# A squared-ReLU MLP by seven products of 2x2 blocks, its hidden activations passing through DRAM

## The chip, the cores and the metric

The kernel runs on one core of a Trainium2 chip. The metric is the device time of one execution in microseconds (us). A core has five engines that run at the same time and wait for one another by semaphores: TensorE (PE; its weight loads are shown as PEld), VectorE (DVE), ScalarE (ACT), GpSimd (POOL) and SyncE (SP, which here only issues DMAs). Each engine works through its own list of instructions in order; a DMA that stands in SP's or ACT's list waits there for its data, and what stands behind it waits too.

## What is computed

One hybrid decoder layer over 1024 tokens (SEQ) of 1024 features (D_MODEL), in float32:

```python
a = rmsnorm(h, g_mix)
conv_out, attn = ...          # gated short convolution and stick-breaking attention from a @ w_in
h = h + concat([conv_out, attn]) @ w_out
m = rmsnorm(h, g_mlp)
h = h + square(relu(m @ w_up)) @ w_down      # w_up 1024 x 4096, w_down 4096 x 1024
gate = sigmoid(rmsnorm(h, g_ple) @ w_ple_gate)
h = h + gate * (p @ w_ple_proj)
return rmsnorm(h, g_final)
```

The change concerns the fifth line, the MLP, and the two seams at which it meets its neighbours.

## The kernel before

Every float32 operand x is kept as two parts in a format that TensorE multiplies in one pass: `hi`, a rounded copy made by ACT, and `lo` = x - hi, made by DVE. `split` (L109) does both. A product is then three matmuls, hi by hi, hi by lo and lo by hi (`product_steps`, L150); each matmul is 128x128 stationary by 128x512 moving, and all terms of a sum go into one PSUM bank of 128x512. There are eight banks under four names (mm, z, tr, av; two each).

SBUF is handed out in units of 4 KB per partition from named groups, the unit that has been free longest first (`Units`, L31). A unit that is given again makes its new writer wait for its last reader.

The layer runs in this order: embedding projection, mixer norm, projections and attention (filled with work that is ready), output projection, MLP, gate. `out_second` (L825) is the second half of the output projection; for each of eight row tiles of 128 tokens it finishes the residual `h1[tt]`, which stays in SBUF until the end. Beside it `Turned` (L225) makes the MLP's input: `norm` scales a row tile on ACT and sends it to DRAM, `back` fetches it with the features spread over the partitions, `turn` finishes the transpose with four DVE transposes, and `split` multiplies by the gain and makes hi and lo. Tokens are handled in halves of 512 (h = 0 and 1): `up` for half 0 needs tiles 0 to 3 only.

The MLP goes through the 4096 hidden features in 16 groups of 256 (two blocks f of 128). `up` multiplies a group for both halves of the tokens and makes the squared ReLU as hi and lo (two ACT and two DVE instructions for each bank of 512 tokens); `down_tile` multiplies the group's 256 features by w_down for a row tile and adds the bank to `h1` with one DVE instruction. `up` of a group and `down` of the group before alternate:

```python
for g in range(2, NG):
    raw = load_up(g + 1) if g + 1 < NG else None
    wd = load_down(g)
    hid = up_units()
    for h in range(NH):
        up(hid, wu, h)
    if raw:
        wu = split_up(raw)
        down(hid_prev, wd_prev)
        hid_prev, wd_prev = hid, wd
```

The last two groups of `down` run tile by tile, with the next `Turned` (for the gate) beside them: tiles 0 to 3 are finished first, and the gate's products begin with them. The order on the engines is set by a scheduler, except on PE in the attention and on DVE in this last stretch of `down`, where it is that of the code.

## Time and profile before

| | |
|---|---|
| median of 3 runs | 1317.72 us (1317.48 to 1318.93) |
| the profiled execution: span from its first to its last instruction | 1314.3 us |
| PE busy | 1280.6 us, 97% |
| DVE, ACT, POOL busy | 827.1, 485.4, 228.9 us (63%, 37%, 17%) |
| mean granted TensorE clock | 0.998 of 2.4 GHz |

The span is what the profile of one execution shows; the runs' times hold 3.4 us more at the median (1317.72 - 1314.3). Busy PE means that matmuls are in flight: the line of a group gives their number and the mean of one from start to end, which is longer than the distance from one to the next. A wait is the idle time of an engine before an instruction and what ended it.

### The profile page before, as it was taken

The page shows a single profiled execution, that of the slowest core. Times are in us where ns is not written, and L with a number is a line of the kernel's source. Part 1 is how long each engine was busy: PE and PEld are TensorE (multiplying, and loading weights), DVE is VectorE, ACT ScalarE, POOL GpSimd, SP SyncE. Part 2 cuts the span into 40 slices and gives each one's busy share as a digit, 9 for nine tenths or more (in the row PEclk, how much of TensorE's full clock was granted, in tenths as well). Part 3 has the DMA queues.
Part 4 walks back from the last instruction along what each step waited for, and adds up shares of the span by engine and source line. Part 5 has one row for each costly group of instructions (what it writes and reads, how often), then busy time and mean ns, then how long its engine had stood idle before and what let it go on. Part 6 is the DMA issues. An engine that isn't in the chain of part 4 may idle for free.

```text
span 1314.3 us, 15437 instructions
## 1 busy us (share of the span) xinstructions
PE 1280.6 (97%) x5981; PEld 1062.9 (81%) x5981; DVE 827.1 (63%) x1248; ACT 485.4 (37%) x835; POOL 228.9 (17%) x248
## 2 busy tenths in 40 slices
PE   8999999999998999999999999999999999999997
...
GB/s 343 186 32 49 34 32 33 33 32 33 49 64 160 49 33 221 121 76 65 52 29 49 64 61 20 49 64 64 17 49 65 64 16 48 33 64 161 240 128 64
DMA packets 71377, 100.11 MB, mean 76 GB/s; under 512 B 4596, under 2 KB 52744, under 8 KB 71304
## 3 DMA queue, kind: packets, MB, share of 16 engines
...
## 4 chain that ended last, share of the span: by engine, by line
PE 71%; DVE 13%; DMA 5%; ACT 3%; issue 3%; POOL 2%; SPq 0%; ACTq 0%; POOLq 0%; DVEq 0%
PE ps_mm L155 37%; PE ps_z L155 11%; PE ps_tr L155 10%; PE ps_av L155 9%; DVE u L591 2%; PE ps_tr L605 1%; PE ps_av L635 1%; DMA u<-n_d 1%; DVE u L111 1%; DVE u L611 1%; PE ps_z L576 1%; DMA u<-in_w_ple_gate 1%; DMA n_d<-u 1%; DVE u L586 1%; DVE u L270 1%
## 5 line engine op out<-in xcount | busy, mean ns | idle before, releaser
L155 PE MATMUL ps_mm<-u,u 128*128 128x512 f32 x3000 | 716.8, 391 | 8.0 <-DVE u L218 2.6
L155 PEld LDWEIGHTS ps_mm<-u,u 128*128 128x128 f32 x3000 | 556.3, 188 | 123.8 <-DVE u L218 3.0
L110 ACT CAST u<-u 128x1024 fp32r<-128x1024 f32 x114 | 119.4, 1051 | 360.3 <-DVE u L111 279.4
L155 PE MATMUL ps_z<-u,u 128*128 128x512 f32 x792 | 198.7, 389 | 0.0
L155 PEld LDWEIGHTS ps_z<-u,u 128*128 128x128 f32 x792 | 148.6, 188 | 30.9
L857 DVE TENSOR_TENSOR u<-u 128x512 f32<-128x512 f32 x64 | 44.2, 691 | 201.3 <-ACT u L855 201.3
L155 PE MATMUL ps_tr<-u,u 128*128 128x512 f32 x660 | 164.5, 389 | 0.0
L155 PE MATMUL ps_av<-u,u 128*128 128x512 f32 (+1 forms) x660 | 161.9, 385 | 0.4 <-DVE u L139 0.4
L111 DVE TENSOR_TENSOR u<-u,u 128x1024 fp32r<-128x1024 f32 x102 | 129.7, 1273 | 38.4 <-ACT u L110 36.9
L155 PEld LDWEIGHTS ps_tr<-u,u 128*128 128x128 f32 x660 | 123.8, 188 | 25.7
L155 PEld LDWEIGHTS ps_av<-u,u 128*128 128x128 f32 x660 | 122.2, 188 | 25.6 <-DVE u L139 0.8
L120 POOL TENSOR_SCALAR me<-ms 128x1 f32<-128x1 f32 x24 | 7.5, 314 | 749.5 <-ACT u L115 749.0
L855 ACT ACTIVATE u<-ps_mm 128x512 f32<-128x512 f32 x62 | 37.0, 597 | 178.5 <-PE ps_mm L155 178.1
L593 POOL TENSOR_TENSOR u<-u,u 128x383 f32<-128x383 f32 (+5 forms) x72 | 72.9, 1015 | 108.3 <-DVE u L591 69.5
L591 DVE TENSOR_TENSOR_SCAN u<-u 128x128 f32<-128x128 f32 (+3 forms) x88 | 83.6, 950 | 2.3 <-ACT u L578 0.3
L884 DVE TENSOR_TENSOR u<-ps_z,u 128x512 f32<-128x512 f32 x88 | 60.6, 689 | 32.1 <-PE ps_z L155 31.2
L884 DVE TENSOR_TENSOR u<-ps_av,u 128x512 f32<-128x512 f32 x74 | 51.0, 689 | 37.5 <-PE ps_av L155 37.5
L884 DVE TENSOR_TENSOR u<-ps_tr,u 128x512 f32<-128x512 f32 x74 | 51.0, 689 | 35.0 <-PE ps_tr L155 34.9
L635 PEld LDWEIGHTS ps_av<-u,u 128*128 128x128 f32 x320 | 50.3, 189 | 22.4 <-DVE u L611 15.3
L635 PE MATMUL ps_av<-u,u 128*128 128x256 f32 (+1 forms) x320 | 54.6, 283 | 11.8 <-DVE u L611 11.4
L610 ACT CAST u<-ps_tr 128x512 fp32r<-128x512 f32 (+1 forms) x80 | 43.4, 543 | 58.2 <-PE ps_tr L605 57.6
L270 DVE STREAM_TRANSPOSE u<-u 128x256 f32<-128x256 f32 x80 | 46.4, 639 | 19.6 <-DMA u<-m_d 10.6
...
## 6 DMA issues: line engine op xcount, KB each, us to landing
u<-in_w_up SPq DMA_DIRECT2D x32, 512.0 KB, 3.4
u<-in_w_down SPq DMA_DIRECT2D x32, 512.0 KB, 3.5
u<-in_w_in SPq DMA_DIRECT2D x24, 512.0 KB, 4.1
u<-in_x SPq DMA_DIRECT2D x16, 512.0 KB, 8.2
pp_d<-u SPq DMA_DIRECT2D x8, 512.0 KB, 6.4
u<-in_w_out SPq DMA_DIRECT2D x8, 512.0 KB, 3.8
m_d<-u ACTq DMA_DIRECT2D x8, 512.0 KB, 2.9
u<-m_d SPq DMA_DIRECT2D x32, 128.0 KB, 3.2
```

Of the source, the lines that this page charges most:

```text
L110: nc.scalar.copy(out=hi, in_=raw)
L111: (eng or nc.vector).tensor_tensor(out=lo, in0=raw, in1=f32(hi), op=ALU.subtract)
L155: nc.tensor.matmul(ps, a, b, start=(i == 0), stop=(i == n - 1))
L270: nc.vector.transpose(self.raw[h][k][0][:, :, i * P:(i + 1) * P].rearrange("p t (b j) -> p t b j", b=4), by_tile[:, 2 * k:2 * k + 2])
L576: nc.tensor.matmul(z[:, :s1 - s0], q[:, tb * P:(tb + 1) * P], k[:, s0:s1], start=(j == 0), stop=(j == 1))
L591: nc.vector.tensor_tensor_scan(out=rev, data0=rev, data1=rev, initial=keep[:, s1:s1 + 1], op0=ALU.mult, op1=ALU.bypass)
L593: (nc.vector if s0 > 0 and pr < 3 else nc.gpsimd).tensor_tensor(out=beta[:, s0:e], in0=beta[:, s0:e], in1=keep[:, s0 + 1:e + 1], op=ALU.mult)
L610: nc.scalar.copy(out=ah[:, :w], in_=tp[:, :w])
L635: nc.tensor.matmul(av[:, t0:256], v, part[:, c0:c0 + 256 - t0], start=(j == 0 and part is ah), stop=(j == n - 1 and part is al))
L855: nc.scalar.activation(rr, ps, AF.Relu)
L857: nc.vector.tensor_tensor(out=s2, in0=rr, in1=rr, op=ALU.mult)
L884: nc.vector.tensor_tensor(out=h1[tt][0][:, ds_], in0=ps, in1=h1[tt][0][:, ds_], op=ALU.add)
```

## The change

The MLP's two products are written in the form of Strassen and Winograd: both operands are cut into 2x2 blocks, sums and differences of blocks are formed, and seven block products (P1 to P7) take the place of eight. What was one sweep over 16 groups is two:

- **up** runs through all 16 blocks n of 256 hidden features. The input m is held as seven block matrices `M` (B11, B21, B22 and the sums T1 to T4), each 4 units in hi and lo. The eighth block, B12, is needed in the sums alone. Each of the seven products of a block is a chain of 12 matmuls in a PSUM bank. P6, P7 and P4 go on adding to the bank of P1 after ACT has copied what stands in it, and P3 goes on adding to that of P5 after DVE has added it to another block. DVE and ACT then build the four blocks of the hidden activations and DVE their three sums; seven slices of 512 tokens go to DRAM (`hs_d`, 1.8 MB for each n).
- **down** runs through 32 steps (8 groups of two n by 4 token tiles `tau` of 128, each step with two row tiles, tau and tau + 4). A step loads for both n the seven slices of its 128 tokens (448 KB in pieces of 512 bytes), splits them, and does seven chains of 6 matmuls; after each, one DVE instruction adds the bank to a half of a row tile of `h1`, which was itself sent to DRAM after the output projection and fetched again.
- the weights are prepared block by block (`prep_up`, `prep_down`): four block sums on POOL, then four splits on ACT and DVE (one of 512, three of 1024 elements).
- PE's order from the output projection to the last chain is that of the code. The row tiles are finished in the order 0, 4, 1, 5, 2, 6, 3, 7 in the last four steps, and the gate takes them in that order.

```diff
+    def prep_up(r):
+        a11, a21 = r[0][0][:, :, 0:P], r[0][0][:, :, P:256]
+        a12, a22 = r[1][0][:, :, 0:P], r[1][0][:, :, P:256]
+        one = W(F32R, (P, 2, 4, P))
+        split(a11, one[0][:, 0], one[0][:, 1])
+        hi, lo = W(F32R, (P, 4, 256)), W(F32R, (P, 4, 256))
+        split(r[1][0], hi[0], lo[0])
...
+        s, q = W(F32, (P, 2, 4, P)), W(F32, (P, 2, 4, P))
+        add(s[0][:, 0], a21, a22, nc.gpsimd)
+        sub(s[0][:, 1], s[0][:, 0], a11, nc.gpsimd)
+        sub(q[0][:, 0], a11, a21, nc.gpsimd)
+        sub(q[0][:, 1], a12, s[0][:, 1], nc.gpsimd)
+        free(*r)
+        for u, names in ((s, ("P5", "P6")), (q, ("P7", "P3"))):
+            hi_, lo_ = W(F32R, (P, 2, 4, P)), W(F32R, (P, 2, 4, P))
+            split(u[0], hi_[0], lo_[0])
...
+    def up(n, name):
...
+        chain(ps, [(lh(t), ll(t), rh(t), rl(t)) for t in range(4)], name in FRESH)
+        held.used()
+        if name == "P1":
+            s["A"] = W(F32, (P, 2, HB))
+            nc.scalar.copy(out=s["A"][0][:, 0], in_=ps)
+        elif name == "P2":
+            a11 = s["A"][0][:, 0]
+            add(a11, ps, a11)
+            relu2(a11)
+        elif name == "P6":
+            nc.scalar.copy(out=s["A"][0][:, 1], in_=ps)
+        elif name == "P7":
+            s["B"] = W(F32, (P, 2, HB))
+            a22 = s["B"][0][:, 0]
+            nc.scalar.copy(out=a22, in_=ps)
+            add(a22, s["V"], a22)
+            relu2(a22)
+        elif name == "P3":
...
+            add(a21, ps, a21)
+            relu2(a21)
+            s["C"], s["D"] = W(F32, (P, 2, HB)), W(F32, (P, 2, HB))
+            c, d = s["C"][0], s["D"][0]
+            add(c[:, 0], a21, a22)
+            sub(c[:, 1], c[:, 0], a11)
+            sub(d[:, 0], a11, a21)
+            for src, i, w in ((a11, 0, HB), (c.rearrange("p a b -> p (a b)"), 1, S)):
+                nc.sync.dma_start(out=hs_d[n * P:(n + 1) * P, i * HB:i * HB + w], in_=src)
+        elif name == "P4":
+            a12, c, d = s["B"][0][:, 1], s["C"][0], s["D"][0]
+            nc.scalar.activation(a12, ps, AF.Relu)
+            nc.vector.tensor_tensor(out=a12, in0=a12, in1=a12, op=ALU.mult)
+            sub(d[:, 1], a12, c[:, 1])
+            for src, i in ((d, 3), (s["B"][0], 5)):
+                nc.sync.dma_start(out=hs_d[n * P:(n + 1) * P, i * HB:(i + 2) * HB],
+                                  in_=src.rearrange("p a b -> p (a b)"))
...
+        gained(1)
+        (b11, b21), (b12, b22) = [(mT.raw[h][0:2], mT.raw[h][2:4]) for h in range(2)]
...
+        t1 = combine(sub, b12, b11)
+        free(*b11)
+        m_block("T1", t1)
+        up(2, "P1")
+        up(2, "P2")
+        t2 = combine(sub, b22, t1)
...
+        for n in range(3):
+            up(n, "P5")
...
+        for n in range(3, NP_):
+            m = n + 1
+            more = m < NP_
+            up(n, "P6")
+            if more:
+                up(m, "P1")
+                up(m, "P2")
+            up(n, "P7")
+            if m + 1 < NP_:
+                ups[m + 1] = prep_up(raws.pop(m + 1))
+                if m + 2 < NP_:
+                    raws[m + 2] = load_up(m + 2)
+            if more:
+                up(m, "P5")
+            up(n, "P3")
+            up(n, "P4")
...
+    def load_hidden(n, tau):
+        r = W(F32, (P, 7, P))
+        nc.sync.dma_start(out=r[0], in_=hs_d[n * P:(n + 1) * P].rearrange("f (i t) -> f i t", i=7)
+                          [:, :, tau * P:(tau + 1) * P])
+        hi, lo = W(F32R, (P, 7, P)), W(F32R, (P, 7, P))
+        split(r[0], hi[0], lo[0])
...
+    def down(k, name):
...
+        chain(ps, ops, name in FRESH)
...
+        top, low = h1[tau][0], h1[tau + 4][0]
+        out_ = {"P1": top[:, 0:HB], "P2": top[:, 0:HB], "P6": top[:, HB:S], "P3": top[:, HB:S],
+                "P4": low[:, 0:HB], "P5": low[:, HB:S], "P7": low[:, HB:S]}[name]
+        add(out_, ps, out_)
...
+    nT = Turned(h1, G_PLE, n_d, "W", "W", ORDER, "W")
...
+        for k in range(last + 1):
+            ahead(k)
+            down(k, "P6")
+            if k < last:
+                down(k + 1, "P1")
+                down(k + 1, "P2")
+            down(k, "P7")
+            if k < last:
+                down(k + 1, "P5")
+            down(k, "P3")
+            down(k, "P4")
+            g, tau = steps_[k]
+            if g == NP_ // GP - 1:
...
+                if tau:
+                    nT.turn(tau - 1)
+                    nT.turn(tau + 3)
+                nT.norm(tau)
+                nT.norm(tau + 4)
+    for k_ in range(4):
+        nT.split(0, k_)
```

`prep_down` has the form of `prep_up`; `relu2` is one DVE instruction, max(x, 0) times x. In the rows that follow a name's second number counts buffers and has no meaning of its own. L111 is the subtraction in `split`, L817 and L820 are `add` and `sub` of the changed kernel (L817 with a `ps_` operand takes a PSUM bank out), L900 is `relu2`.

**Where the output projection meets up, DVE.** Before, the last `turn` (tile 7, L270) is followed by the splits of half 1 (L279), between squared-ReLU work of the first groups (L857, L858):

```order
L270 STREAM_TRANSPOSE u450_4923<-u461_4998 128x2x128
L270 STREAM_TRANSPOSE u451_4924<-u461_4998 128x2x128
L270 STREAM_TRANSPOSE u452_4925<-u461_4998 128x2x128
L270 STREAM_TRANSPOSE u453_4926<-u461_4998 128x2x128
L279 SCALAR_TENSOR_TENSOR u474_5110<-u450_4923,gp_91,u473_5109 128x512 x2
L279 SCALAR_TENSOR_TENSOR u476_5116<-u451_4924,gp_91,u475_5115 128x512 x2
L279 SCALAR_TENSOR_TENSOR u478_5122<-u452_4925,gp_91,u477_5121 128x512 x2
L857 TENSOR_TENSOR u472_5100<-u472_5100 128x512
L279 SCALAR_TENSOR_TENSOR u480_5128<-u453_4926,gp_91,u479_5127 128x512 x2
```

In the changed kernel the last transpose of tile 7 (L272) is followed by the lo part of a weight block, P2 of block 2, and the sums T1, T2 and T3 (L820); the two rows with which this piece ends are the lo parts of T1:

```order
L272 STREAM_TRANSPOSE u454_4946<-u462_5015 128x2x128
L111 TENSOR_TENSOR u484_5131<-u480_5121,u483_5130 128x1024
L817 TENSOR_TENSOR u493_5171<-ps_av_5173,u493_5171 128x512
L820 TENSOR_TENSOR u487_5146<-u451_4943,u426_4714 128x1024
L820 TENSOR_TENSOR u488_5147<-u452_4944,u427_4715 128x1024
L900 SCALAR_TENSOR_TENSOR u493_5171<-u493_5171 128x512
L820 TENSOR_TENSOR u494_5188<-u453_4945,u487_5146 128x1024
L820 TENSOR_TENSOR u451_4943<-u453_4945,u451_4943 128x1024
L820 TENSOR_TENSOR u495_5189<-u454_4946,u488_5147 128x1024
L820 TENSOR_TENSOR u452_4944<-u454_4946,u452_4944 128x1024
L111 TENSOR_TENSOR u491_5152<-u487_5146,u489_5150 128x1024
L111 TENSOR_TENSOR u492_5153<-u488_5147,u490_5151 128x1024
```

Work that took no part in the seam before (four block sums) now stands between the last transpose and T1, which the first P5 multiplies.

**In the steady part of up, DVE.** Before, one stretch of a group reads so (L884 is the bank of `down`, L111 a weight's lo part):

```order
L884 TENSOR_TENSOR u415_4552<-ps_av_7087,u415_4552 128x512
L111 TENSOR_TENSOR u631_7116<-u629_7113,u630_7115 128x1024
L884 TENSOR_TENSOR u415_4552<-ps_z_7095,u415_4552 128x512
L857 TENSOR_TENSOR u636_7148<-u636_7148 128x512
L858 TENSOR_TENSOR u633_7120<-u636_7148,u632_7119 128x512
L111 TENSOR_TENSOR u641_7244<-u624_7103,u640_7243 128x1024
```

In the changed kernel P2 of one block is taken out, squared, two lo parts of weights follow, and then the bank of P5 is added at P7 (the fifth row), which P3 waits for on PE; the last row is P3's own bank:

```order
L817 TENSOR_TENSOR u574_5857<-ps_av_5859,u574_5857 128x512
L900 SCALAR_TENSOR_TENSOR u574_5857<-u574_5857 128x512
L111 TENSOR_TENSOR u582_5904<-u579_5897,u581_5903 128x1024
L111 TENSOR_TENSOR u584_5908<-u580_5898,u583_5907 128x1024
L817 TENSOR_TENSOR u575_5886<-ps_tr_5780,u575_5886 128x512
L900 SCALAR_TENSOR_TENSOR u575_5886<-u575_5886 128x512
L817 TENSOR_TENSOR u559_5722<-ps_tr_5780,u559_5722 128x512
```

The two rows of weights have moved in front of an addition for which PE waits; before, nothing on PE waited for `lo` rows of a weight until a group later.

**Where up meets down, DVE.** Before, `down`'s first banks are taken out between rows of `up` (L884 in the third row):

```order
L111 TENSOR_TENSOR u503_5316<-u489_5176,u502_5315 128x1024
L857 TENSOR_TENSOR u499_5306<-u499_5306 128x512
L884 TENSOR_TENSOR u368_4026<-ps_z_5319,u368_4026 128x512
L858 TENSOR_TENSOR u469_5010<-u499_5306,u468_5009 128x512
L111 TENSOR_TENSOR u508_5454<-u506_5451,u507_5453 128x1024
```

In the changed kernel this is the end of a piece of 30 rows between the last row of block 14 and the first bank of `down` (the last row here); lo parts of weights (1024) and of the hidden slices (896) for the first four steps make up most of it:

```order
L820 TENSOR_TENSOR u713_7196<-u711_7177,u712_7195 128x512
L111 TENSOR_TENSOR u786_7554<-u784_7551,u785_7553 128x896
L111 TENSOR_TENSOR u749_7297<-u745_7287,u748_7296 128x1024
L111 TENSOR_TENSOR u737_7270<-u735_7267,u736_7269 128x896
L111 TENSOR_TENSOR u778_7486<-u776_7483,u777_7485 128x896
L111 TENSOR_TENSOR u772_7422<-u768_7412,u771_7421 128x1024
L111 TENSOR_TENSOR u740_7276<-u738_7273,u739_7275 128x896
L817 TENSOR_TENSOR u714_7220<-ps_z_7300,u714_7220 128x512
```

The bank of P1 of the first step is taken out behind all of them, and P6, which adds to the same bank, stands behind that on PE.

## Rows read from the trace of the kernel before

**Rows 1.** The page's first part: busy us, share, count of each engine.

```profile
PE 1280.6 (97%) x5981; PEld 1062.9 (81%) x5981; DVE 827.1 (63%) x1248; ACT 485.4 (37%) x835; POOL 228.9 (17%) x248
```

**Rows 2.** Chain that ended last, a step in the MLP: start, us, engine, bank.

```profile
587.61 21.76 PE ps_mm L155 x96
```

**Rows 3.** Windows: busy us of each engine, clock, DMA share, GB/s.

```profile
core 0: us, PE busy (x) PEld busy (x) DVE busy (x) ACT busy (x) POOL busy (x), PEclk, DMA share, GB/s
500.00:550.00 50.00, 49.48 (x218) 40.46 (x217) 39.81 (x65) 29.18 (x42) 3.93 (x11) 1.00 0.62 189
1000.00:1050.00 50.00, 50.00 (x222) 41.42 (x221) 25.45 (x34) 11.54 (x16) 0.00 (x0) 1.00 0.20 69
1200.00:1250.00 50.00, 49.77 (x219) 40.55 (x217) 39.74 (x62) 28.30 (x43) 4.72 (x12) 1.00 0.70 211
150.00:200.00 50.00, 47.92 (x260) 40.48 (x259) 45.64 (x81) 29.19 (x58) 20.45 (x19) 1.00 0.11 32
```

**Rows 4.** Groups by form, 600 to 1150: busy us, mean ns of one.

```profile
L111 DVE TENSOR_TENSOR u<-u,u 128x1024 fp32r<-128x1024 f32 x51 | 62.4, 1224 | 7.4 <-ACT u L110 6.5
L110 ACT CAST u<-u 128x1024 fp32r<-128x1024 f32 x51 | 53.6, 1051 | 280.6 <-DVE u L111 256.4 <-DMA u<-in_w_down 12.6 <-DVE u L858 11.6
L884 DVE TENSOR_TENSOR u<-ps_z,u 128x512 f32<-128x512 f32 x77 | 53.1, 690 | 27.0 <-PE ps_z L155 26.1
```

**Rows 5.** Timeline of PE, 454 to 465, rows of the output projection among attention's.

```profile
454.76 0.62 PE L155 MATMUL ps_z<-u,u 128*128 128x512 f32 x2
...
464.58 0.39 PE L155 MATMUL ps_z<-u,u 128*128 128x512 f32 x1
```

**Rows 6.** Groups by form, 488 to 552, where the MLP's input is made.

```profile
L270 DVE STREAM_TRANSPOSE u<-u 128x256 f32<-128x256 f32 x32 | 18.7, 643 | 10.7 <-DMA u<-m_d 10.6
...
L278 ACT ACTIVATE u<-u,gp 128x512 fp32r<-128x512 f32 x16 | 10.2, 711 | 6.5 <-DVE u L270 6.1 <-ACT u L240 0.4
L240 ACT ACTIVATE u<-u,rs 128x1024 f32<-128x1024 f32 x8 | 9.1, 1149 | 4.9 <-POOL rs L123 4.9
L115 ACT ACTIVATE u<-u 128x1024 f32<-128x1024 f32 x8 | 8.5, 1057 | 14.7 <-DVE u L715 9.0 <-DMA m_d<-u 5.2 <-DVE u L270 0.5
```

**Rows 7.** DMA issues: count, KB each, median us from issue to landing.

```profile
u<-in_w_up SPq DMA_DIRECT2D x32, 512.0 KB, 3.4
...
m_d<-u ACTq DMA_DIRECT2D x8, 512.0 KB, 2.9
u<-m_d SPq DMA_DIRECT2D x32, 128.0 KB, 3.2
n_d<-u ACTq DMA_DIRECT2D x8, 512.0 KB, 3.9
u<-n_d SPq DMA_DIRECT2D x32, 128.0 KB, 3.4
```

**Rows 8.** Windows around an idle stretch of PE, columns as in rows 3.

```profile
400.00:404.00 4.00, 1.73 (x11) 1.22 (x9) 3.98 (x6) 0.63 (x3) 2.84 (x4) 1.00 0.45 131
404.00:406.00 2.00, 2.00 (x9) 1.71 (x7) 1.99 (x1) 2.00 (x5) 2.00 (x1) 0.60 0.03 8
406.00:408.00 2.00, 2.00 (x8) 1.60 (x8) 1.93 (x4) 1.17 (x2) 2.00 (x2) 0.55 0.36 106
```

**Rows 9.** Timeline, 565 to 567: a chain of six and its bank's addition.

```profile
565.69 1.52 PE L155 MATMUL ps_z<-u,u 128*128 128x512 f32 x6
567.48 0.68 DVE L884 TENSOR_TENSOR u<-ps_z,u 128x512 f32<-128x512 f32 x1
```

**Rows 10.** Timeline of POOL and DVE, 391 to 401.

```profile
391.00 1.09 POOL L593 TENSOR_TENSOR u<-u,u 128x511 f32<-128x511 f32 x1
393.75 6.36 POOL L111 TENSOR_TENSOR u<-u,u 128x1024 fp32r<-128x1024 f32 x2 [0.55 <-ACT u L110]
...
394.56 3.31 DVE L524 SCALAR_TENSOR_TENSOR u<-u,gc,u 128x1022 f32<-128x1022 f32 x1
397.79 0.55 DVE L611 TENSOR_TENSOR u<-ps_tr,u 128x384 fp32r<-128x384 f32 x1
398.26 2.94 DVE L111 TENSOR_TENSOR u<-u,u 128x1024 fp32r<-128x1024 f32 x1
```

More of the change, by code (lines that the diff above doesn't have):

```diff
@@ L225, in hybrid_layer_kernel, with __init__ @@
     class Turned:
-        def __init__(self, src, gcol, hn_d, raw="A", row="R"):
+        def __init__(self, src, gcol, hn_d, raw="A", row="R", order=range(8), out="A"):
+            self.order, self.out_group = list(order), out
             self.src, self.gcol, self.hn_d, self.raw_group, self.row_group = src, gcol, hn_d, raw, row
@@ L263, in turn @@
         def turn(self, tt):
-            h, i = tt // 4, tt % 4
+            at = self.order.index(tt)
+            h, i = at // 4, at % 4
             if i == 0:
@@ L794, in split_half, with W @@
         return a, b
-    G = 2
-    NG = 32 // G
-    def load_up(g):
-        r = [U.get("W", F32, (P, 4, 256)) for _ in range(2)]
+    for f in SECOND[len(y2):]:
+        y2.append(split_unit(Y[f], "VY"))
+    for g in list(U.free_q):
+        if g != "W":
+            U.move(g, "W", len(U.free_q[g]))
+    NP_ = 16
+    h_d = dpool.tile([S, D], F32, name="h_d")
+    hs_d = dpool.tile([NP_ * P, 7 * HB], F32, name="hs_d")
+    mm_steps = product
+    def W(dtype, shape=(P, S)):
+        return U.get("W", dtype, shape)
@@ new lines, in free, with add, sub, __init__ @@
+    def free(*us):
+        for u in us:
+            U.put(u, "W")
+    def add(out, a, b, eng=None):
+        (eng or nc.vector).tensor_tensor(out=out, in0=a, in1=b, op=ALU.add)
+    def sub(out, a, b, eng=None):
+        (eng or nc.vector).tensor_tensor(out=out, in0=a, in1=b, op=ALU.subtract)
+    class Held:
+        def __init__(self, units, uses):
+            self.units, self.left = units, uses
+        def used(self):
+            self.left -= 1
+            if not self.left:
+                free(*self.units)
@@ new lines, in hybrid_layer_kernel, with new_bank, chain @@
+    RIGHT = {"P1": "B11", "P2": "B21", "P5": "T1", "P6": "T2", "P7": "T3", "P3": "B22", "P4": "T4"}
+    FRESH = ("P1", "P2", "P5")
+    BANKS = {"X": ("mm", "z"), "V": ("tr", "av")}
+    turns = {"X": 0, "V": 0}
+    def new_bank(kind):
+        turns[kind] += 1
+        return bank(BANKS[kind][turns[kind] % 2])
+    def chain(ps, ops, fresh):
+        n = 3 * len(ops)
+        i = 0
+        for lh, ll, rh, rl in ops:
+            for a, b in ((lh, rh), (lh, rl), (ll, rh)):
+                nc.tensor.matmul(ps, a, b, start=(fresh and i == 0), stop=(i == n - 1),
+                                 skip_group_check=not fresh)
+                i += 1
@@ L825, in out_second @@
+    mT = Turned(h1, G_MLP, m_d, raw="W", row="W")
+    raws = {n: load_up(n) for n in range(2)}
     def out_second(tt):
@@ new lines, in hybrid_layer_kernel, with ahead @@
+    ORDER = (0, 4, 1, 5, 2, 6, 3, 7)
+    nT = Turned(h1, G_PLE, n_d, "W", "W", ORDER, "W")
+    wg = []
+    def ahead(k):
+        if k + 1 < len(steps_):
+            g, tau = steps_[k + 1]
+            hidden[k + 1] = [load_hidden(g * GP + p_, tau) for p_ in range(GP)]
+        g, tau = steps_[k]
+        if (g + 1) * GP < NP_:
+            if tau in (0, 2):
+                dr.append(load_down((g + 1) * GP + tau // 2))
+            else:
+                n = (g + 1) * GP + tau // 2
+                downs[n] = prep_down(dr.pop(0))
```

301 lines of the change are left out of this document (169 added, 132 removed).

## The prediction

> **What bounds the kernel now.** The first view is the page's table of busy time [rows 1]: PE is busy for 97% of the span, DVE for 63%, ACT 37%, POOL 17%. The chain that ended last tells why: through the MLP it is matmuls alone, 96 of them in 21.76 us [rows 2], so one matmul costs 21.76 / 96 = 0.2267 us. The windows say where the other engines have room [rows 3]: in the middle of the MLP (1000 to 1050) PE is busy for all 50 us, DVE for 25.45, ACT for 11.54, POOL for none. At both of the MLP's ends PE is nearly full as well, 49.48 of 50 us where the MLP's input is made and 49.77 where the gate begins: seams that cost nothing. So time is saved here only by fewer matmuls, and lost only where PE is made to wait.
>
> **The change part by part.** Times are of the profiled execution, 1314.3 us; the runs' median is 3.4 us above it, which is added at the end.
>
> *Fewer matmuls.* Before, up and down have 16 x 96 = 1536 matmuls each. After, up has 16 x 7 x 12 = 1344 and down 32 x 7 x 6 = 1344. 384 fewer by 0.2267 us [rows 2] is **-87.0**. The rest of the sum is what PE waits for.
>
> *Attention's tail.* Before, the output projection's second half already fills holes of the attention: 16 matmuls between 454.76 and 464.58 [rows 5], 3.6 us. In code order they come afterwards. Bounds 0 and 3.6, and the holes are partly others' anyway: **+2**.
>
> *Front seam.* I follow PE's new row order from the first matmul of `out_second` (time 0). PE has eight tiles of 24 matmuls (43.5 us) and six chains of 12 (P1 and P2 of three blocks, 16.3): 59.8. P1(0) waits for B11's lo parts, which queue on DVE among transposes and evictions (2.3 by the row order), and P1(2) for a weight's lo part (3.1): the cover ends at 65.2. P5(0) needs T1, and T1 needs tile 7. Its residual is there at 44.2; on ACT some 10 us of casts and gains (1.05 and 0.71 each [rows 4, 6]) stand ahead of its norm; norm, scaling and pass through DRAM take 1.06 + 0.5 + 1.15 [rows 6] + 2.9 + 3.2 [rows 7] = 8.8; two lo parts ahead 2.4 and four transposes by 0.643 [rows 6] 2.6: 68.0. Then 1.4 of gain, and on DVE six sums, a relu2 and two lo parts, 6 x 1.224 + 0.69 + 2 x 1.224 [rows 4] = 10.5: 79.9, 14.7 after the cover ends. Before, half 0 alone was enough to begin; T1 is a difference of both halves. After idle PE runs slow for a while: after the gap at 400 to 404 the granted clock was 0.60 and 0.55 for the next 4 us [rows 8], at those shares 1.7 us lost, called 2. With 1.4 less for gaps that were there before: 2.3 + 3.1 + 14.7 + 2 - 1.4 = **+21** (16 to 26, by the queue's length on ACT).
>
> *Steady up.* A block takes PE 84 x 0.2267 = 19.04 us. DVE, ACT and POOL need 12.3, 6.2 and 4.4 of these, by the durations of [rows 4] and POOL's 1.09 for a sum of 512 [rows 10]. PE has one tight spot: P3 adds to the bank of P5 and must wait until DVE has added that bank to another block. In DVE's order this addition stands behind the eviction and squaring of P2 and two lo parts of weights. P2's matmuls are through at 8.16 us of the cycle (three chains of 2.72); with 0.43 us of latency [rows 9], then 0.69 + 0.69 + 1.22 + 1.22 + 0.69, it ends at 13.1, and P3 is due after five chains, at 13.6: some 0.4 us of slack. What takes it is POOL. When POOL and DVE both work on SBUF they don't overlap freely: two POOL subtractions of 1024 took 6.36 us while a DVE instruction took 3.31, and a DVE lo part beside the second took 2.94 where 1.224 is usual; a DVE copy out of PSUM between them kept its 0.55 [rows 4, 10]. In up, POOL's four sums for the block after the next start when the second raw weight tile lands. Its load (3.4 us [rows 7]) stands on SP behind the writes of the hidden blocks and lands 9 to 11 us into the cycle, right where those lo parts run. A stall is between 0 and 2.7 us per block; each of up to three SBUF instructions of DVE can be held by up to 1.09, half of it on average, less the slack: about 1.0, in some 12 blocks, **+12** (0 to 30).
>
> The Trainium skill, SBUF — State Buffer, section Who interferes with whom, says that GpSimd and DVE share a port pair under an exclusive lock, that a DVE instruction with two SBUF inputs contends with a GpSimd instruction that reads SBUF, and one with at most one SBUF input doesn't. The trace agrees: 2.94 against 1.224 us, and 0.55 unchanged [rows 10]. It speaks against this change, whose sums on POOL all read SBUF; by it the sum stays where it is, without it POOL's part of the terms would be 0 and the sum that of the first rival.
>
> *Mid seam.* 30 rows stand on DVE between the last row of block 14 and the first bank of down, most of them lo parts of 1024 (1.224) and of 896 (1.09, interpolated between 0.69 and 1.224 [rows 4]): 28.8 us. P6 of step 0 adds to the bank of P1 and waits for them: it starts 34.8 us after P4(14), where PE has 15 us of chains: 19.8. Twelve POOL sums run beside these rows (+4), the clock falls once (+2 [rows 8]), and block 15's share of up's stalls is counted here (-2): **+24** (17 to 32).
>
> *Down.* Four steps take PE 28 x 6 x 0.2267 = 38.1 us. DVE has in them 28 evictions by 0.69 [rows 4], eight lo parts of hidden slices by 1.09, and two weight blocks by 0.69 + 3 x 1.224: 19.3 + 8.7 + 8.7 = 36.7, 96% of PE's time and in fixed order. P7 and P4 wait for the eviction three chains earlier, P6 for one six earlier, P3 for one eight earlier. Walking the 28 chains with these waits and 0.43 us of latency [rows 9] gives 40.5 us per group. POOL's eight sums hold DVE by some 0.4 each after what is hidden: about 43. Some six of the eight groups are full (the first has its blocks ready, the last prepares none): 6 x 2.4 = 15 without POOL's part, 6 x 4.7 = **+28** with it. Bounds: 6 (DVE's rests hidden, one stall per group) to 60 (every sum holds DVE for its whole 1.09).
> The loads are no limit: a step reads 896 KB in 9.5 us, 95 GB/s, with the weights 150; pieces of 512 bytes moved 32 GB/s at a share of 0.11 in the last row of [rows 3], about 290 at a full share.
>
> *Tail.* The gate's first half needs tiles 0, 4, 1, 5; from the last addition to tile 5 PE has two steps of cover, 19 us. Behind it come two norms (1.06 + 1.15 each with POOL's power between), out and back (3.9 + 3.4 [rows 7]), eight transposes (5.1), eight splits, and turns stand ahead of evictions on DVE, which holds PE earlier. The walk has the first gate product at 46.5 where 30.6 would be without waits; with the clock **+17** (10 to 22).
>
> Sum: 1314.3 - 87.0 + 2 + 21 + 12 + 24 + 28 + 17 = 1331.3; with 3.4, **1335 us**. The saving goes into three seams (62) and into DVE's fixed order (40).
>
> **Rivals.**
> *POOL's sums cost nothing:* they fall beside evictions, which POOL doesn't disturb [rows 10], or into DVE's rests. Then up 0, mid 20, down 15: -87 + 2 + 21 + 0 + 20 + 15 + 17 = -12, **1306 us, faster**. This is the one that ends on the other side. Its place is P3's wait in up and P7's and P4's in down; it decides when all stalls by POOL come to less than about 13 us, 0.3 us per block in up and 1 per group in down. For it: DVE is 65% busy in up. Against: in down 96%.
> *The seams are half hidden and down keeps PE's pace:* half of 62, nothing else beyond 5: -87 + 31 + 5 = -51, **1267 us**. For it: before, the seams cost almost nothing [rows 3]. Against: T1 and the 30 rows can't be earlier in DVE's order.
> *POOL and DVE run strictly one after the other:* up's stall 2.7 by 15, down 60: -87 + 2 + 24 + 40 + 28 + 60 + 19 = +86 less 18 where POOL waits behind DVE instead, **1386 us**.
>
> **How the numbers follow.** The forecast has a chance of 0.55 (its own range 1320 to 1352), the free POOL 0.29 (1295 to 1318), half-hidden seams 0.07, the serial case 0.09. A measurement here tells about 0.2%, 2.6 us, from no change. Faster: 0.07 + 0.26 of the second case (its upper edge reaches no change): 0.33. Same: 0.03 of that case and 0.05 of the forecast's lower edge, 0.08. Slower: 0.50 + 0.09 = 0.59. The range, 1280 to 1372, leaves out most of the two extreme cases (0.16 together) and a little of the forecast's upper tail.
>
> **What the profile after would show.** PE idle of 15 to 20 us before P5(0), released by DVE's lo part of T1; of some 20 us before P6 of step 0, released by the first L817 of down; of 10 us or more before the gate. In up a cycle of 20 us, not 19.04, with idle before P3 released by the L817 of P7's addition; L111 on DVE well above 1.224 us there. In down a group of four steps of 43 us, PE waiting for L817. Granted clock below 1 after each long gap. POOL's sums above 1.09. Wrong would be: L111 at 1.22 and POOL at 1.09 beside each other (then 1306), seams below 8 us each, or SP's queue, not DVE, as what ended PE's waits.

## Result and the profile after

The changed kernel takes 1362.72 us (median of 4 runs, 1359.1 to 1366.45) against 1318.33 for the kernel before: ratio 1.0335 (95% interval 1.0311 to 1.036), slower by 44.4 us where 17 were forecast. The sign was right and the size was not. Its profiled execution spans 1363.0 us, 48.7 more than the one before.

The page's first part, of after, answers to [rows 1]:

```profile
PE 1229.8 (90%) x5597; PEld 1004.3 (74%) x5597; DVE 1035.4 (76%) x1414; ACT 565.7 (42%) x913; POOL 439.7 (32%) x376
```

PE does 384 matmuls less and is busy for 51 us less, yet the span has grown. So the time is in waits of PE, and in slower matmuls behind some of them. Its list of waits, of after (what waited, for which engine and line, us in all, times, the longest):

```profile
PE ps_z L895 <- ACT u L110: 32.3, 4, 19.5
PE ps_tr L895 <- DVE u L817: 23.3, 13, 5.1
...
PE ps_z L895 <- DVE u L817: 8.4, 6, 1.9
PE ps_tr L895 <- ACT u L110: 7.0, 1, 7.0
PE ps_z L895 <- DVE u L111: 6.4, 2, 4.4
```

L895 is the matmul of `chain`. Thirteen waits for L817 are P3's, one in nearly every block; the long ones for L110 (a split's cast) are the seams. A number in brackets behind a product is its block: P5(0) is P5 of block 0. To see what each stage lost I take the time between two matmuls and subtract 0.2267 us for each matmul between them. The landmarks are rows of PE's timeline of after:

```profile
522.23 2.88 PE L155 MATMUL ps_av<-u,u 128*128 128x512 f32 x12
531.24 0.79 PE L895 MATMUL ps_z<-u,u 128*128 128x512 f32 x1 [6.13 <-ACT u L110]
...
571.68 5.06 PE L895 MATMUL ps_tr<-u,u 128*128 128x512 f32 x11 [4.10 <-DVE u L111]
...
892.57 2.88 PE L895 MATMUL ps_mm<-u,u 128*128 128x512 f32 x12
914.96 1.22 PE L895 MATMUL ps_z<-u,u 128*128 128x512 f32 x2 [19.50 <-ACT u L110]
920.60 0.79 PE L895 MATMUL ps_z<-u,u 128*128 128x512 f32 x1 [4.42 <-DVE u L111]
925.16 1.92 PE L895 MATMUL ps_z<-u,u 128*128 128x512 f32 x3 [3.77 <-ACT u L110]
926.88 2.66 PE L895 MATMUL ps_av<-u,u 128*128 128x512 f32 x6
...
1265.94 0.73 PE L155 MATMUL ps_mm<-u,u 128*128 128x512 f32 x2 [3.83 <-ACT u L280]
```

The first is the end of the output projection (525.0); 571.45 is where P5(0)'s first matmul would begin if it stood right ahead of the other eleven; 895.3 is the end of up, 926.88 the second chain of down, 1265.94 the gate. For the front seam that is 571.45 - 524.95 - 6 x 2.72 = 30.2. In the same way, for after and for the runs that are told below (us that PE lost; "down" ends 16 chains before the gate):

| run | front | up | mid | down | tail |
|---|---|---|---|---|---|
| forecast | 21 | 12 | 24 | 28 | 17 |
| after | 30.2 | 35.5 | 30.2 | 17.2 | 18.5 |
| no sums | 23.9 | 5.7 | 16.5 | 8.4 | 19.8 |
| sums on POOL, unused | 26.6 | 37.0 | 28.9 | 36.3 | 19.3 |
| sums on DVE | 22.9 | 9.9 | 24.4 | 13.8 | 19.8 |
| P4 first | 29.5 | 7.2 | 29.3 | 15.4 | 18.5 |
| w_up loads on ACT | 28.5 | 50.7 | 30.4 | 13.6 | 18.5 |
| sums on DVE, P4 first | 23.6 | 5.4 | 28.9 | 15.6 | 18.9 |

One block of up shows the mechanism. First DVE's timeline, of after, then POOL's and one row of ACT's, in the same stretch:

```profile
759.12 0.69 DVE L820 TENSOR_TENSOR u<-u 128x512 f32<-128x512 f32 x1
759.72 2.31 DVE L111 TENSOR_TENSOR u<-u,u 128x1024 fp32r<-128x1024 f32 x1
761.96 1.77 DVE L820 TENSOR_TENSOR u<-u,u 128x512 f32<-128x512 f32 x1
763.65 0.68 DVE L944 TENSOR_TENSOR u<-u 128x512 f32<-128x512 f32 x1
764.37 1.67 DVE L820 TENSOR_TENSOR u<-u,u 128x512 f32<-128x512 f32 x1
767.53 0.69 DVE L817 TENSOR_TENSOR u<-ps_av,u 128x512 f32<-128x512 f32 x1 [1.50 <-PE ps_av L895]
...
771.25 2.42 DVE L111 TENSOR_TENSOR u<-u,u 128x1024 fp32r<-128x1024 f32 x2 [2.30 <-ACT u L110]
773.58 0.68 DVE L817 TENSOR_TENSOR u<-ps_tr,u 128x512 f32<-128x512 f32 x1
```

```profile
759.34 1.60 POOL L817 TENSOR_TENSOR u<-u,u 128x512 f32<-128x512 f32 x1 [12.97 <-PE ps_z L895]
761.02 2.16 POOL L820 TENSOR_TENSOR u<-u,u 128x512 f32<-128x512 f32 x1
763.86 1.62 POOL L820 TENSOR_TENSOR u<-u 128x512 f32<-128x512 f32 x1 [0.68 <-issue]
765.44 1.74 POOL L820 TENSOR_TENSOR u<-u,u 128x512 f32<-128x512 f32 x1
```

```profile
770.16 2.24 ACT L110 CAST u<-u 128x1024 fp32r<-128x1024 f32 x2 [4.83 <-DMA hs_d<-u]
```

POOL's four sums begin as soon as P4 of the block is through (a unit comes free then), not when a weight tile lands. Beside them a lo part takes 2.31 us instead of 1.22 and two subtractions 1.77 and 1.67 instead of 0.69: each loses about what a sum of POOL takes alone, 1.09 [rows 10], 3.15 us per block. The rows that I had expected to be held (771.25) run at their usual 1.21 each, but late: they waited 2.30 us for ACT's cast, and the cast 4.83 us for a write of hidden activations to DRAM (`hs_d`). The chain that ended last, of after, from the block before, shows how the loss gets there (start, us, what):

```profile
739.00 2.23 DVE u L111
741.22 1.71 DVE u L820
742.95 0.32 SPq L940
...
743.38 0.38 SPq L836
...
743.85 5.47 DMA hs_d<-u
...
749.42 1.06 ACT u L110
...
750.51 2.36 DVE u L111 x2
752.87 0.61 DVE u L817
...
753.53 3.03 PE ps_tr L895 x12
```

A held lo part and a held subtraction make the hidden block late, and with it its writes: L940, and L947, which stands behind L940 and a load of w_up (L836) in SP's list. L947's write lands 5.47 us after its issue, and only then the cast begins; it makes a part of the weights in a unit that the hidden block has held until then. Two lo parts, the addition of P7, and only then P3. The casts do not wait for the load of w_up. ACT's waits of after, from 600 to 850:

```profile
ACT u L110 <- DMA hs_d<-u: 51.2, 15, 5.2
...
ACT u L110 <- DMA u<-in_w_up: 4.2, 2, 2.7
```

The load counts in another way, beside the write. One block later than the last load of w_up, rows of DVE are held for as long as in the block above (2.31, 1.78 and 1.67 us), but the cast begins 3.5 us after L947's issue (848.31), and P3 waits for 0.32 us and not for 1.5:

```profile
851.82 2.21 ACT L110 CAST u<-u 128x1024 fp32r<-128x1024 f32 x2 [2.54 <-DMA hs_d<-u]
...
857.13 3.01 PE L895 MATMUL ps_tr<-u,u 128*128 128x512 f32 x12 [0.32 <-DVE u L817]
```

A block takes 20.8 to 22.4 us instead of 19.04, this last one aside.

### The profile page after: what moved, and what is told of

It reads as the page before. It is cut to its first block, busy times and chain, and to the rows that moved or that the text cites. A ratio compares the mean times of both kernels' runs of the same rounds, so it can differ in the third digit from the quotient of the medians.

```text
span 1363.0 us, 15562 instructions
## 1 busy us (share of the span) xinstructions
PE 1229.8 (90%) x5597; PEld 1004.3 (74%) x5597; DVE 1035.4 (76%) x1414; ACT 565.7 (42%) x913; POOL 439.7 (32%) x376
## 4 chain that ended last, share of the span: by engine, by line
PE 39%; DVE 20%; issue 16%; DMA 10%; POOL 8%; ACT 4%; SPq 1%; POOLq 0%; ACTq 0%; DVEq 0%
PE ps_mm L155 16%; DVE u L111 7%; POOL u L820 6%; PE ps_tr L895 5%; DMA hs_d<-u 5%; DVE u L820 3%; PE ps_tr L155 3%; PE ps_z L155 3%; PE ps_av L155 3%; PE ps_mm L895 2%; DVE u L817 2%; PE ps_z L895 2%; DVE u L593 2%; PE ps_av L637 2%; ACT u L110 2%
## 5 line engine op out<-in xcount | busy, mean ns | idle before, releaser
L110 ACT CAST u<-u 128x1024 fp32r<-128x1024 f32 (+2 forms) x256 | 242.2, 970 | 405.8 <-POOL u L820 103.6
L155 PE MATMUL ps_mm<-u,u 128*128 128x512 f32 (+1 forms) x1464 | 365.1, 395 | 10.2 <-ACT u L280 3.8
L111 DVE TENSOR_TENSOR u<-u,u 128x1024 fp32r<-128x1024 f32 (+2 forms) x244 | 305.7, 1268 | 72.5 <-ACT u L110 70.0
L155 PEld LDWEIGHTS ps_mm<-u,u 128*128 128x128 f32 x1464 | 269.4, 190 | 65.5 <-ACT u L280 4.2
L895 PE MATMUL ps_z<-u,u 128*128 128x512 f32 x768 | 200.7, 404 | 47.5 <-ACT u L110 32.3
L895 PE MATMUL ps_tr<-u,u 128*128 128x512 f32 x756 | 190.6, 402 | 34.4 <-DVE u L817 23.3
L895 PEld LDWEIGHTS ps_z<-u,u 128*128 128x128 f32 x768 | 147.7, 194 | 86.7 <-ACT u L110 34.1
L895 PE MATMUL ps_mm<-u,u 128*128 128x512 f32 x768 | 192.9, 393 | 13.0 <-ACT u L110 5.7
L895 PEld LDWEIGHTS ps_tr<-u,u 128*128 128x128 f32 x756 | 145.2, 194 | 71.3 <-DVE u L817 28.8
L895 PEld LDWEIGHTS ps_mm<-u,u 128*128 128x128 f32 x768 | 144.5, 189 | 47.4 <-DVE u L817 6.5
L820 POOL TENSOR_TENSOR u<-u,u 128x512 f32<-128x512 f32 x80 | 137.8, 1732 | 38.3 <-DMA hs_d<-u 35.6
L820 POOL TENSOR_TENSOR u<-u 128x512 f32<-128x512 f32 x32 | 47.3, 1480 | 236.3 <-PE ps_mm L895 137.5
L895 PE MATMUL ps_av<-u,u 128*128 128x512 f32 x396 | 101.7, 401 | 0.0
L817 DVE TENSOR_TENSOR u<-ps_tr,u 128x512 f32<-128x512 f32 x95 | 63.6, 684 | 45.9 <-PE ps_tr L895 41.1
L895 PEld LDWEIGHTS ps_av<-u,u 128*128 128x128 f32 x396 | 77.7, 196 | 16.8
L817 POOL TENSOR_TENSOR u<-u,u 128x512 f32<-128x512 f32 x16 | 25.2, 1573 | 200.4 <-PE ps_z L895 79.3
L637 PEld LDWEIGHTS ps_av<-u,u 128*128 128x128 f32 x320 | 50.1, 189 | 24.9 <-DVE u L613 18.1
L637 PE MATMUL ps_av<-u,u 128*128 128x256 f32 (+1 forms) x320 | 54.8, 284 | 13.7 <-DVE u L613 13.2
L272 DVE STREAM_TRANSPOSE u<-u 128x256 f32<-128x256 f32 x80 | 46.1, 635 | 26.1 <-DMA u<-m_d 19.8
```

The source lines that it names most:

```text
L110: nc.scalar.copy(out=hi, in_=raw)
L111: (eng or nc.vector).tensor_tensor(out=lo, in0=raw, in1=f32(hi), op=ALU.subtract)
L155: nc.tensor.matmul(ps, a, b, start=(i == 0), stop=(i == n - 1))
L272: nc.vector.transpose(self.raw[h][k][0][:, :, i * P:(i + 1) * P].rearrange("p t (b j) -> p t b j", b=4), by_tile[:, 2 * k:2 * k + 2])
L637: nc.tensor.matmul(av[:, t0:256], v, part[:, c0:c0 + 256 - t0], start=(j == 0 and part is ah), stop=(j == n - 1 and part is al))
L817: (eng or nc.vector).tensor_tensor(out=out, in0=a, in1=b, op=ALU.add)
```

## Experiments

**No sums on POOL.** In `prep_up` and `prep_down` the four sums go, and the raw tiles are split in their place (the result is then not the layer's); `prep_up` is shown:

```diff
-        add(s[0][:, 0], a21, a22, nc.gpsimd)
-        sub(s[0][:, 1], s[0][:, 0], a11, nc.gpsimd)
-        sub(q[0][:, 0], a11, a21, nc.gpsimd)
-        sub(q[0][:, 1], a12, s[0][:, 1], nc.gpsimd)
-        free(*r)
-        for u, names in ((s, ("P5", "P6")), (q, ("P7", "P3"))):
+        for u, names in ((r[0], ("P5", "P6")), (r[1], ("P7", "P3"))):
...
```

> The 128 block sums on POOL are left out (up and down); the two raw tiles of a block are split in their place, so the weights of P3, P5, P6, P7 (in down P4 to P7) are not the right ones, with the same casts, lo parts and matmuls. Theory lock: DVE's SBUF instructions beside POOL cost 1.05 to 1.1 us more each, 3.1 us per block in up, 8 us in the mid seam; without them up has a cycle of 19.3 us instead of 20.9, the mid seam shrinks from 30 to about 20, a group of down from 40.1 to 39: about 1325 us, L111 at 1.22 and L820 at 0.69 all through. Theory queue: P3 waits because the weight tile is loaded behind the hidden blocks' writes; the order on SP stays, so the cycle stays above 20.3 and the time above 1345. Theory fixed order (DVE's list, not POOL): above 1350.

Measured: 1304.1 us, 0.9893 (0.9879 to 0.9908): 58.6 us less than the changed kernel, more than theory lock had, and theory queue is out: SP's order did change, but one load of w_up goes out as P6's copy begins (729.18 and 729.38) and the other only 7.7 us after it (737.07), where it was 4.5 in the block above, and still P3 waits no more between 600 and 845 us. The windows from 600 to 850, of this run and then of after, have PE busy for 247.88 and 228.41 of 250 us:

```profile
600.00:850.00 250.00, 247.88 (x1087) 204.66 (x1085) 144.91 (x194) 74.66 (x102) 0.00 (x0) 0.99 0.49 175
```

```profile
600.00:850.00 250.00, 228.41 (x975) 185.00 (x974) 176.16 (x180) 70.63 (x95) 85.49 (x50) 0.98 0.40 141
```

The 128 sums on POOL cost, by stage, 6.3 us in the front seam, 29.8 in up, 13.7 in the mid seam and 8.8 in down (the table's second row less the third), and nothing in the tail. But the run differs in three more things: casts need no sums, a block holds two units less, and the scheduler has ordered DVE anew. One lo part, and not two, stands ahead of P7's addition (the second row):

```profile
736.99 1.23 DVE L111 TENSOR_TENSOR u<-u,u 128x1024 fp32r<-128x1024 f32 x1 [0.68 <-ACT u L110]
738.22 0.69 DVE L817 TENSOR_TENSOR u<-ps_tr,u 128x512 f32<-128x512 f32 x1
```

The next run tells the first apart, and the run with the sums on DVE, which has all the units in use and is nearly as fast in up, speaks against the second. The order was not varied by itself: it has one lo part ahead of that addition in the three runs in which up is short (no sums, sums on DVE, P4 first), and two in the changed kernel and in the next run.

**The same sums on POOL, used by nobody.** As above, with the four POOL instructions put back (the diff is against the run above); weights are still split from the raw tiles, so no instruction waits for a sum's value, though a unit still comes free only when POOL has read it.

```diff
+        s, q = W(F32, (P, 2, 4, P)), W(F32, (P, 2, 4, P))
+        add(s[0][:, 0], a21, a22, nc.gpsimd)
...
+        free(s, q)
         for u, names in ((r[0], ("P5", "P6")), (r[1], ("P7", "P3"))):
```

> POOL makes all its block sums as in the changed kernel, but nobody uses them: the weights are split from the raw tiles, as in the run without sums (1304.1 us), so nothing waits for a result of POOL and its adds stand in nobody's way but the port's. Theory lock: DVE is held as before, and most of the 58.6 us between the two runs come back: above 1340 us, L820 and L111 on DVE at 1.5 us or more in up. Rival, the wait for POOL's results (its sums are late, so casts and lo parts are): the time stays below 1312.

Measured: 1380.41 us, 1.0471 (1.0451 to 1.049). All of it came back, and 18 us more, mostly in down. Theory lock holds: nobody need wait for a sum's value for POOL's work to cost this. DVE's groups by form, from 620 to 860, of this run:

```profile
L111 DVE TENSOR_TENSOR u<-u,u 128x1024 fp32r<-128x1024 f32 x33 | 51.9, 1588 | 28.5 <-ACT u L110 28.5
L820 DVE TENSOR_TENSOR u<-u,u 128x512 f32<-128x512 f32 x22 | 37.8, 1720 | 0.4
...
L817 DVE TENSOR_TENSOR u<-ps_tr,u 128x512 f32<-128x512 f32 x24 | 16.5, 688 | 32.8 <-PE ps_tr L896 32.8
```

and of the run without sums, where the same rows read

```profile
L111 DVE TENSOR_TENSOR u<-u,u 128x1024 fp32r<-128x1024 f32 x34 | 41.5, 1221 | 10.7 <-ACT u L110 10.7
...
L820 DVE TENSOR_TENSOR u<-u,u 128x512 f32<-128x512 f32 x24 | 16.4, 685 | 0.1
```

L820 between two SBUF operands takes 1720 ns against 685; L817 out of PSUM takes 688 here and 692 there. That POOL stretches these rows is so shown; that the stretch reaches P3 is shown by the chain above. How up's 29.8 us divide between the stretch and the second lo part in front of the addition is not: by the rows of the block above (an estimate) the two held rows are 2.2 us longer (2.31 and 1.77 against 1.22 and 0.69), more than P3's usual wait of 1.5 us, and a lo part is 1.22, somewhat less than it. Why this run is slower than the changed kernel itself was not followed.

**The sums on DVE.** `nc.gpsimd` is left out of the eight calls, so that DVE makes the sums.

```diff
-        add(s[0][:, 0], a21, a22, nc.gpsimd)
+        add(s[0][:, 0], a21, a22)
...
```

> All block sums of the weights run on DVE instead of POOL, four of 0.69 us for each block. Theory lock: POOL's sum stops DVE for about 1.08 us, more than the 0.69 that DVE needs itself, so up and the mid seam get no worse and rather better: 1340 to 1360 us. Rival, DVE as the bound: 2.76 us more on DVE per block in up and per block in down (two per group: 36.7 + 5.5 = 42.2 us of DVE against 38.1 of PE), so a group of down goes to 43 or more and the time to 1370 to 1385.

Measured: 1320.79 us, 1.0021 (1.0011 to 1.0031): 41.9 us faster than the changed kernel, better than theory lock had. To do the work itself takes DVE 0.68 us for a sum; to have POOL do it beside it cost up to 1.09. A group of down goes at 39.8 us (977.42 to 1017.24 between the same waits), not 43: the rival, DVE as the bound, is out, although DVE works 5.5 us more.

**P4 ahead of P3 in up.** P4's part takes ReLU and square only, the sums and writes follow P3; shown is the loop, the first three blocks change likewise:

```diff
-            up(n, "P3")
             up(n, "P4")
+            up(n, "P3")
```

> In up P4 runs ahead of P3, so that the addition of P5's bank at P7, for which P3 waits, has one chain (2.72 us) more. Theory: up's 1.85 us per block are P3's wait alone, for whatever reason that addition is late; they go, some 12 blocks, and the clock's dips in up with them: a cycle of 19.1 to 19.4 us, 1335 to 1342 us. Rival: the wait only moves (to P6 or P1 of the next block, whose banks DVE or ACT then frees later, or to the last block's hidden slices, which are written 2.7 us later, at the mid seam): above 1352.

Measured: 1331.63 us, 1.0099 (1.0084 to 1.0114), 31.1 us faster than the changed kernel. Up falls from 35.5 to 7.2 us while POOL still works 80.57 us beside it: POOL still stretches rows of DVE (L817 with both operands in SBUF takes 1442 ns on average from 620 to 860, and 692 without sums), and one chain of slack keeps it from PE. The window from 600 to 850, of this run:

```profile
600.00:850.00 250.00, 249.31 (x1100) 206.12 (x1099) 169.47 (x198) 72.72 (x102) 80.57 (x49) 1.00 0.47 169
```

**Loads of w_up issued by ACT.**

```diff
-            nc.sync.dma_start(out=r[k][0], in_=w_up[:, n * 256:(n + 1) * 256]
+            nc.scalar.dma_start(out=r[k][0], in_=w_up[:, n * 256:(n + 1) * 256]
```

> The loads of w_up are issued by ACT instead of SP, so that they no longer stand behind the writes of the hidden blocks, which wait for DVE. Theory queue: the second raw tile lands 3 to 5 us earlier, its lo parts no longer stand late in front of the addition at P7, P3's wait of 1.5 us goes: about 1340 us with POOL's sums as they are. Theory lock alone: POOL's sums still stretch DVE, and the time stays above 1355.

Measured: 1372.46 us, 1.0412 (1.0396 to 1.0427), slower by 9.7. In ACT's list the two loads stand behind two copies out of PSUM: in the block whose P6 ends at 766.8 they go out at 766.84 and 769.56, 0.0 and 2.7 us after the start of P6's copy. In the block of the changed kernel shown above it is 2.2 and 4.5 us (764.18 and 766.48, the copy at 762.02). So the loads are some 2 us earlier in the block, and yet up lost 50.7 us instead of 35.5: an earlier load does not shorten P3's wait, and theory queue fails here too. The casts ahead of P3 wait for the writes of the hidden block again:

```profile
774.02 1.05 ACT L110 CAST u<-u 128x1024 fp32r<-128x1024 f32 x1 [3.88 <-DMA hs_d<-u]
776.95 1.05 ACT L110 CAST u<-u 128x1024 fp32r<-128x1024 f32 x1 [1.88 <-DMA hs_d<-u]
```

The second ends 11.2 us after P6's copy begins, where it was 10.4 (770.16 and 2.24, less 762.02), and P3's wait grows from 1.46 to 2.24 us. The load now runs beside the second write; that it makes this write late fits the block without a load, but was not tried by itself.

**Sums on DVE and P4 first together.**

> Sums on DVE and P4 ahead of P3 together. Alone they gave 41.9 and 31.1 us. In up both remove the same waits of P3 (35.5 us of waits in the changed kernel, 9.9 and 7.2 with one of the two): theory, they overlap, up comes to about 5 us, the seams and down stay as with the sums on DVE: 1312 to 1318 us. Rival: two separate losses, which add up: 1290 to 1297.

Measured: 1322.23 us, 1.0031 (1.0019 to 1.0043), no better than the sums on DVE alone, and above the range of the theory. The two remedies take away the same loss, in up (9.9, 7.2 and 5.4 us); against the sums on DVE alone the mid seam is 4.5 us longer and down 1.8.

**Hidden slices ahead of h1.** On top of the last one, `hidden[0]` gets its units first and the loads of the eight row tiles of h1 come last before the first chain:

```diff
-    del h1[:]
-    for tt in range(8):
-        h1.append(W(F32))
-        nc.sync.dma_start(out=h1[tt][0], in_=h_d[tt * P:(tt + 1) * P])
...
+        hidden[0] = [load_hidden(p_, 0) for p_ in range(GP)]
         dr = [load_down(0)]
```

> As the one before, and where down begins the hidden slices and weights of the first step take the units that are free first, ahead of the eight row tiles of h1 (which are needed only when the first bank is taken out). Theory: the mid seam is long because the first hidden slices wait for units that block 15 still holds, so that their loads stand behind its writes on SP; the seam shrinks by 8 to 15 us. Rival: the 30 rows on DVE ahead of the first bank set it; then less than 3 us.

Measured: 1312.82 us, 0.9956 (0.9939 to 0.9974): 9.4 us less than the run before it, and the first version with all its sums that is faster than the kernel before. The first chain of down no longer waits; PE's waits move to the next two, for casts and lo parts of weights and then (879.16) for casts of hidden slices:

```profile
865.09 0.80 PE L895 MATMUL ps_av<-u,u 128*128 128x512 f32 x1 [6.87 <-ACT u L110]
870.50 1.22 PE L895 MATMUL ps_av<-u,u 128*128 128x512 f32 x2 [4.61 <-DVE u L111]
879.16 0.79 PE L895 MATMUL ps_tr<-u,u 128*128 128x512 f32 x1 [6.16 <-ACT u L110]
```

So units and SP's order had a part, some 9 us. The three waits that are left, 17.6 us, are for ACT's casts and DVE's lo parts; how much of them DVE's 30 rows set was not tried.

**Another order of the last eight steps.** On top of sums on DVE and P4 first; the loads of the last weights, the turns and the gate's weights are moved to fit, the last to the end of step 29, behind the gate's first splits:

```diff
-    steps_ = [(g, tau) for g in range(NP_ // GP) for tau in range(4)]
+    steps_ = [(g, tau) for g in range(6) for tau in range(4)]
+    steps_ += [(g, tau) for half in ((0, 1), (2, 3)) for g in (6, 7) for tau in half]
```

> Sums on DVE, P4 first, and the last eight steps of down in another order: token tiles 0 and 1 of both last groups first, so that row tiles 0, 4, 1, 5 are finished four steps (38 us) before the gate instead of two. Theory: the tail's 18.5 us are the way of tile 5 through norm, DRAM, turn and split, for which two steps are too short; with four they fall to 3 or less, while the last group's weights are prepared within two steps and cost some 4 us: 10 to 15 us faster than the run with sums on DVE and P4 first. Rival: DVE's list, with turns and splits in front of evictions, sets the tail whatever the cover: less than 4 us.

Measured: 1337.81 us, 1.0149 (1.0127 to 1.0171), 15.6 us slower than the version that it was made from. PE waits for casts of the gate's weights, which come late,

```profile
PE ps_mm L155 <- ACT u L110: 11.6, 2, 7.6
```

and from the gate's first matmul to the end it takes 121.7 us instead of 96.8; 13 of the difference are 58 matmuls of down that now run behind that first matmul. Whether units run short, with two groups' weights held at once, or the gate's weights are late by their new place alone was not followed, and whether more cover alone would help is left open.

**The gate's weights one step later.** Sums on DVE, P3 ahead of P4, hidden slices ahead of h1, and:

```diff
-                if tau == 1:
+                if tau == 2:
                     U.free_q["G"] = deque()
```

> Sums on DVE, P3 ahead of P4 as in the changed kernel, hidden slices ahead of h1 at the start of down, and the gate's weights take their units one step later, behind the hidden slices of the last step. Theory: in the tail PE waits twice (5.3 and 3.2 us) for the last step's hidden slices, whose units stand in line behind the gate's weights; these waits go and the tail falls from 19.8 to 10 to 13; with 9 us of the mid seam, from the 1320.8 us of the run with sums on DVE: 1302 to 1308. Rival: the gate's own weights are then late, and the tail only changes its name: 1310 to 1315.

Measured: 1309.02 us, 0.9941 (0.9928 to 0.9954), between the two ranges: the tail falls from 19.8 to 10.5 us as the theory had it, 2 us come back behind the gate's start (99.3 against 97.7).

**The same with P4 first.**

> As the one before, with P4 ahead of P3. Theory: without sums on POOL nothing of P3's wait is left that another order could save, so the two agree within 4 us. Rival: each change of order is worth its own part, 5 us or more.

Measured: 1308.88 us, 0.9932 (0.992 to 0.9945). The two agree; P4 first is worth nothing once POOL is quiet.

**The kernel before, with POOL sums beside its MLP.** In `split_up`, for each of the two tiles:

```diff
+            for j in range(4):
+                nc.gpsimd.tensor_tensor(out=r[k][0][:, :, 0:P], in0=r[k][0][:, :, 0:P], in1=r[k][0][:, :, P:256],
+                                        op=ALU.add)
             U.put(r[k])
```

> The kernel before, and beside its MLP the same number of POOL additions as in the changed kernel (128 of 512 elements, both operands in SBUF) whose results nobody uses. Theory: the lock stretches DVE's lo parts here too (1.4 us or more instead of 1.22 where they meet), but DVE is busy for half of the time and PE waits for none of these rows within a group, so the time stays within 5 us of 1318. Rival: a POOL sum costs PE time wherever it stands, as in the changed kernel (58.6 us for 128): 1345 or more.

Measured: 1322.35 us, 1.0033 (1.002 to 1.0046), 4.9 us for the same 128 sums that cost the changed kernel 58.6. The window from 600 to 1150 and DVE's groups in it, of this run:

```profile
600.00:1150.00 550.00, 550.00 (x2428) 455.44 (x2427) 293.33 (x356) 117.69 (x155) 151.76 (x104) 1.00 0.14 48
```

```profile
L111 DVE TENSOR_TENSOR u<-u,u 128x1024 fp32r<-128x1024 f32 x52 | 74.1, 1426 | 4.5 <-ACT u L110 3.7
L861 DVE TENSOR_TENSOR u<-u,u 128x512 fp32r<-128x512 f32 x52 | 52.8, 1016 | 4.8 <-DVE u L860 0.9
```

L111 rises from 1224 ns [rows 4] to 1426, DVE's busy time by 25.6 us (267.70 in the same window of the kernel before), and PE is busy for all 550 us in both. DVE's rows are stretched here too; no matmul in this window waits for them.

## Why the prediction was right and wrong

*Fewer matmuls, -87.0:* as forecast (PE has 5597 instructions instead of 5981).

*Attention's tail, +2:* the output projection ends 4.8 us later (524.95 against 520.13); 3.6 of it are the 16 matmuls [rows 5], the upper bound. The other 1.2 are within what this date differs by among the runs, whose attention is the same (522.8 to 526.3).

*Front seam, +21:* 30.2 less 1.4, 28.8. The mechanism was right (P5(0) waits for T1's casts and lo parts), the sizes were not: P5(0) waited 7.0 and 4.1 us, where 14.7 were worked out, and P1(0) 6.1 and 1.9, where 2.3 were. Left out was that POOL's sums for the weights of blocks 1 and 2 run in this very stretch, 6.3 us by the run without them: five lo parts took 8.40 us at 534.44, by the usual 1.224 6.1. The clock's low stretches, called 2, came three times, behind the waits for P1(0), P1(2) and P5(0) (granted clock 0.80 and 0.64 in the windows 525 to 550 and 550 to 575): at P1(0) and P5(0) eleven matmuls took 5.06 us, where twelve take 2.88.

*Steady up, +12:* 35.5. This is the step that failed, and with its term the sum. I had the right engine pair, the right addition and the right wait (13 waits of P3 for L817, 23.3 us), but let POOL act only on rows that stand directly in front of that addition: "each of up to three SBUF instructions of DVE can be held by up to 1.09, half of it on average, less the slack: about 1.0" (by these numbers it is 1.2, 15 us in all, which would not have saved the term). The sums begin with the cycle (759.34, where P6 begins at 759.10), and not 9 to 11 us into it when the load lands. They cost three rows 3.15 us, and the loss travels: late hidden block, late writes on SP, a cast that waits until such a write has landed (5.5 us beside the load, 3.5 without one), late lo parts, P3 1.5 us late in a usual block and up to 5.1 in the first ones. I had looked at that queue for when POOL's sums start, which it doesn't decide, and not for what POOL's sums do to it. The runs without sums, with unused sums, with sums on DVE and with P4 first agree on this, with the reserve on DVE's order made above; the run with loads on ACT shows that an earlier load does not help. The rest of the 35.5 us had no term at all: the granted clock was 0.92 to 0.95 in four windows of 25 us, some 6.5 us by these shares (an estimate), and P5(0)'s slow matmuls fall into this stage too.

*Mid seam, +24:* 30.2. A size near enough by a partly wrong path: it is not P6(0) that waits behind the first bank's row on DVE, but P1(0) itself, for hidden slices and weights that come late (19.50, 4.42 and 3.77 us). POOL's part is 13.7 and not 4, if the run without sums is the measure; units and the queue behind h1's loads and block 15's writes are some 9.

*Down, +28:* 17.2, with 40.1 us per group where 43 were forecast and 40.5 without POOL. POOL's part is 8.8 instead of 13. The wait was the right one, and its size was put too high.

*Tail, +17:* 18.5. Right in size by luck, for half of it was not tile 5's way: 9 us went when the last step's hidden slices no longer stood behind the gate's weights for units, which no step of mine had.

The Trainium skill, SBUF — State Buffer, section SBUF: two separate sides, says that a DVE instruction with two SBUF inputs, or a GpSimd instruction that reads SBUF beside it, gets the shared port pair for the whole instruction if it starts first, and that the other fully blocks. The trace agrees: 1.77 instead of 0.69 and 2.31 instead of 1.22, a loss of 1.08 or 1.09 whatever the DVE instruction's own length, and 0.69 for PSUM sources. Had the term been made with the whole length for every sum that meets DVE, as its upper bound had it, the sum would have been nearer.

The first rival (POOL's sums cost nothing, 1306 us) failed in the changed kernel, but the run without sums comes out where it was worked out: 1304.1. In part this is luck: up lost 5.7 us there where the rival has none, down 8.4 where it has 15. What the forecast fell short by, 28 us (1362.72 less 1335), is about what POOL cost beyond its terms: 58.6 measured, 29 in the terms (12, 4 and 13).
